# RWKV-7's chain of states: one product on TensorE's whole array for both heads of a pair

## The chip, the cores and the metric

The kernel runs on one core of a Trainium2 chip. It uses TensorE (PE: matrix products, with its weight loads PEld), VectorE (DVE), ScalarE (ACT), GpSimd (POOL) and SyncE (SP, which issues most transfers). The metric is the device time of one execution in microseconds (us), lower is better, as a median over runs.

## The reference

Two decoder layers work on 256 tokens of 2048 features. Each layer normalises, projects, runs four token mixers side by side (retention, HGRN2, mLSTM, RWKV-7; 8 heads of 64 features each), projects their joined outputs back, and then runs a SwiGLU sub-layer. The change concerns RWKV-7, whose state is one 64 x 64 matrix per head:

```python
def step(state, inp):
    rt, lwt, kt, vt, kkt, at = inp
    state = (state * jnp.exp(lwt)[:, :, None, :]
             - jnp.einsum('bhvk,bhk->bhv', state, kkt)[..., None] * (at * kkt)[:, :, None, :]
             + vt[..., None] * kt[:, :, None, :])
    return state, jnp.einsum('bhvk,bhk->bhv', state, rt)
...
_, y = lax.scan(step, jnp.zeros((b, h, d, d), r.dtype), xs)
```

## The kernel before

**Large products.** Features lie on partitions, tokens on the free axis. Weights stream in from memory in units (`w_raw`, 512 KB); ACT copies each unit's high part (`w_hi`) and DVE subtracts to get the low part (`w_lo`), three units ahead of use. TensorE adds three partial products of high and low parts in PSUM. In a mixing sub-layer the input projection runs first (banks `acc`, operand `u`). Then comes the output projection, whose operands `m` are the high and low parts of the mixers' results `mx`. It takes the results in the order of `MIXED`: `rw0, hg0, ml0, hg1, ml1, rt0, rt1, rw1`. Its first three column groups, 512 wide, go through all eight results together, so that none of the later columns can start before the last results are there.

**Between the large products** `interleave` puts the steps of the mixers: it counts TensorE's own work in `self.pe`, and a step that yields `RLAT` (2.2) is put behind that much other work. The tile scheduler then sets each engine's final order with a timeline of its own. Every engine goes through its order strictly, so a product whose input is late holds up all that stand behind it on TensorE.

**RWKV-7** works on pairs of heads, four pairs per layer, one after the other; the heads of a pair lie on partitions 0 to 63 and 64 to 127 (`half[0]`, `half[1]`). `rw_head` prepares a pair while the pair before it is still at work. `rwkv` takes four chunks of 64 tokens at once up to an inverse of a 64 x 64 triangular block per head and chunk: pairwise products (`pr<-KVR,BK`), inverses of 16 x 16 blocks on DVE with three transfers through memory (`LD`, `XD`; the result is `TDD`), and products that merge them (`pr<-TDD,LoT` and so on) into `TT`. Then the states go from chunk to chunk, for n = 0 to 3:

- kappa step (n > 0): the state `S0[n]` times the chunk's kappa, which lies in `KVR` (`pr<-S,KVR`), added to `MV` by DVE into `F[4]`;
- inverse step: `TT[n]` times that (`pr<-F,TT`; for n = 0, where no state is there yet, `pr<-ra,TT`), written negated into `KVT` as -U, one head by ACT and one by DVE;
- KBT step (n < 3): `KBT[n]` times `KVT[n]` (`pr<-KVT,KBT`), decayed into `S0[n+1]` by DVE with the decayed old state `S0c` from POOL.

Each of these products is issued once per head, with 64 columns of weights; the two land on the two halves of the partitions of one PSUM bank (`R`, two banks in turn, `pr` in the profile). Last come the outputs (`pr<-KVT,G` and `pr<-S,KVR`, also under that name), copied into `kap`, and `rw_tail`: layer norm of each head (reduce, four squares on ACT, a power on POOL, four scalings on DVE), two transposes (`pr<-ident,kap`), gate product (`pr<-SG,gup`), result `mx`, split into `m` by ACT and DVE. All these products are float32; the large ones are float32r. Every product goes through `mm`, line 299, so in the profile they are told apart by their tiles.

Of the kernel before, what the change touches and what calls it, by code (L numbers as in the profile page):

```python
"""Two-layer decoder trunk: four parallel token mixers (retention, HGRN2, mLSTM, RWKV-7) and SwiGLU.

Features of the projections lie on partitions, tokens on the free axis; the residual stream has
tokens on partitions.  Large products split both float32 operands exactly into a high and a low
12-bit part and add the three significant partial products in PSUM.
"""
# [14 lines left out]
AF = mybir.ActivationFunctionType  # L21
ALU = mybir.AluOpType
# [9 lines left out]
# TensorE time (us) that other work fills before the next dependent step of a chain is put in its order  # L32
# [14 lines left out]
# ---------------------------------------------------------------- host layout  # L47
# [6 lines left out]
def _block_cols():  # L54
    """Columns of w_in for each block of 256, in the order the kernel walks them."""
    out = {}
    rw, ml, hg, rt = RW0, ML0, HG0, RET0
    out["lora"] = list(range(rw + 1536, rw + 1792))
    for s in range(2):
        out[f"rwv{s}"] = _tile_cols(rw + 1024, 2 * s) + _tile_cols(rw + 1024, 2 * s + 1)  # L60
    for j in range(4):
        out[f"rw{j}"] = _tile_cols(rw, j) + _tile_cols(rw + 512, j)
        out[f"ml{j}"] = _tile_cols(ml, j) + _tile_cols(ml + 512, j)
        out[f"hg{j}"] = _tile_cols(hg, j) + _tile_cols(hg + 512, j)
        out[f"rt{j}"] = _tile_cols(rt, j) + _tile_cols(rt + 512, j)
    for s in range(2):
        out[f"mlv{s}"] = list(range(ml + 1024 + 256 * s, ml + 1280 + 256 * s))
        out[f"mlo{s}"] = list(range(ml + 1536 + 256 * s, ml + 1792 + 256 * s))
        out[f"hgv{s}"] = list(range(hg + 1024 + 256 * s, hg + 1280 + 256 * s))
        out[f"hgg{s}"] = list(range(hg + 1536 + 256 * s, hg + 1792 + 256 * s))  # L70
        out[f"rtv{s}"] = list(range(rt + 1024 + 256 * s, rt + 1280 + 256 * s))
        out[f"rtg{s}"] = list(range(rt + 1536 + 256 * s, rt + 1792 + 256 * s))
    return out
# [147 lines left out]
# ---------------------------------------------------------------- the program  # L221


class Weights:
    """Streams weight units: load, then split into high and low parts, ahead of their use."""
# [45 lines left out]
class Trunk:  # L271
# [4 lines left out]
    # ---- small helpers  # L276
# [28 lines left out]
    def pw(self, out, a, e):  # L305
        """out = a ** e on GpSimd; e is one of the constant columns."""
        col = {-0.5: self.mhalf}[e]
        n = a.shape[1]
        self.lp = self.nc.gpsimd.tensor_tensor(out=out, in0=a, in1=col.to_broadcast([128, n]), op=ALU.pow)  # L309
# [9 lines left out]
    # ---- setup  # L319
# [49 lines left out]
    # ---- plan of the weight stream  # L369
# [36 lines left out]
    # ---- large products  # L406
    def u_slice(self, k):
        """High and low parts of a feature chunk."""
        u = self.u[k // 2][:, k % 2]
        return u[:, 0, :], u[:, 1, :]  # L410

    def ft_unit(self, acc, k0):
        """Four feature chunks of a block with features on partitions."""
# [11 lines left out]
    def gu_unit(self, accs, k0):  # L425
        """Four feature chunks of a gate and up block, a bank each; the products with the low part apart."""
# [13 lines left out]
    def tf_block(self, accs, ncol=256):  # L440
        """A block with tokens on partitions, a bank for each half of them."""
# [12 lines left out]
    def y_acc(self, bank, bank2=None, wide=False):  # L454
        """Places of the two token halves of a block: one bank, or one each."""
# [3 lines left out]
    def y_unit(self, acc, xs, k0, last):  # L459
        """Adds a weight unit from chunk k0 on; returns the next chunk."""  # L460
# [18 lines left out]
    def halves(self, acc):  # L479
        """A wide block as two of 256 columns."""  # L480
        return [(tuple(o[:, c:c + 256] for o in acc[0]), True) for c in (0, 256)]

    # ---- norms
# [48 lines left out]
    def behind_norm(self):  # L532
        """Keeps work that is ready early out of the norm's way."""
# [5 lines left out]
    def y_stats(self, acc, b, which, yw, final=False):  # L539
        """Scaled block of the sub-layer's output and its shares of the three sums."""  # L540
# [66 lines left out]
    # ---- feed-forward sub-layer  # L607
# [54 lines left out]
    # ---- mixing sub-layer  # L662
# [3 lines left out]
    def mixing(self):  # L666
        tc, nc, A, l = self.tc, self.nc, self.A, self.l
        with ExitStack() as ctx:
# [16 lines left out]
            with self.behind_norm() if l > 0 else nullcontext():  # L685
# [4 lines left out]
                # parameters derived on chip: 1 - mu for the fourteen shifted tiles, 1 - k_a, HGRN bounds  # L690
# [10 lines left out]
                # shared scratch  # L701
# [20 lines left out]
    # ---- order of TensorE's work in the mixing sub-layer  # L722
    def interleave(self):
        """The stream of large products runs through; a step of a mixer goes in between as soon as what
        it waits for should be there.  Times are estimates in microseconds of TensorE's own work."""
# [33 lines left out]
    def stream(self):  # L759
        """Projections, then the output products as far as their inputs are there."""  # L760
# [54 lines left out]
    def settle(self):  # L815
        """Empty the finished blocks whose destinations are free; split finished mixer outputs."""
# [90 lines left out]
    # ---- pieces the mixers share  # L907
    def ssq(self, sq, ps):
        """Per-token, per-head sums of a [feature, token] tile: ps[token, (half, head)]."""
# [3 lines left out]
    def widen(self, rc, rb):  # L913
        """Repeat rc[token, (half, head)] over the features of the head."""
# [12 lines left out]
    def finish(self, j, scale_fn, out):  # L927
        """Normalise each head of the attended values, weigh and gate it."""
# [12 lines left out]
    def attend(self, P, v, j, nw=None):  # L941
        """Sum over source tokens, [feature, token] of the pair's heads; kept squared and weighed."""
# [12 lines left out]
    def scores(self, q, k, hh):  # L955
        """k^T q of one head: [source, (first|second target half of the first source half, second half)]."""
# [6 lines left out]
    def oth_tiles(self, t):  # L963
# [12 lines left out]
        # running maxima, a row for each head: high parts from row 0, low parts from row 32  # L976
# [11 lines left out]
    # ---- retention  # L988
# [48 lines left out]
    # ---- HGRN2  # L1037
    def hgrn_bounds(self, t):
        """Second layer's lower bounds: (p0 + p1) - p0 of the softmax over layers."""
# [39 lines left out]
    def hgrn(self, j, st, v, out):  # L1079
        """Scores by levels: a target in the upper half of 2m tokens meets the sources of the lower half,  # L1080
        both decayed to the middle.  The queries of the pair's heads stand side by side in q2, each on
        its head's features, with zeros on the other's."""
# [4 lines left out]
        # scores within blocks of 64 (source, target) gather in the middle of P, then move to its sides  # L1087
# [7 lines left out]
        e = out  # L1095
# [58 lines left out]
    # ---- mLSTM  # L1154
# [15 lines left out]
    def ml_stats(self):  # L1170
        """Stabiliser quantities of all heads: g = i - F, running maximum M of g and 0, exp(-(F + M))."""
# [44 lines left out]
    def mlstm(self, j, qk, v, out):  # L1216
# [14 lines left out]
        # values and the normaliser (the column of ones) with tokens on partitions  # L1231
# [31 lines left out]
    # ---- RWKV-7  # L1263
    def shift(self, acc, ct, mu, i, out):
        """Mix each token's projection with the one before it."""
# [16 lines left out]
    def vmix(self):  # L1282
        """Mix the first layer's values into this one's."""
# [17 lines left out]
    def rw_tiles(self, t):  # L1301
# [11 lines left out]
        self.TT = t([128, 4, 64], "TT")  # L1313
# [12 lines left out]
    def decay(self, th, p):  # L1326
        """exp(-DECAY * sigmoid(x)) in place from th = tanh(x / 2): (e^-DECAY/4 * exp(z))^2, z = -DECAY/4 * th."""
# [14 lines left out]
    def rw_head(self, j):  # L1342
        """What a pair needs of its projections; runs while the pair before it goes through its states."""
# [15 lines left out]
        # keys of unit length: their squared lengths divide b, where both of its keys come together  # L1359
# [31 lines left out]
    def rwkv(self, j, out):  # L1391
# [8 lines left out]
        for hh in range(2):  # L1400
            self.mul(KVR[half[hh], :, hh, :], c4(kap[half[hh]]), cpd[half[hh], :, 0:64])
            self.act(KVR[half[hh], :, 1 - hh, :], c4(vj[half[hh]]))
        self.mul(KVR[:, :, 2, :], c4(r), cpd[:, :, 1:65])
        yield RWB
        # pairwise products within chunks, rows b (own half) and k (other half), columns kappa and r
# [16 lines left out]
        # token-major copies  # L1422
# [6 lines left out]
        # merge to 32 x 32 and 64 x 64 inverses: products of both heads  # L1429
# [10 lines left out]
        # inverses of the 16 x 16 diagonal blocks, one block per partition  # L1440
# [24 lines left out]
        def quad_mm(lhs, rhs, up):  # L1465
            """32 x 32 products; the results land on the upper (0) or lower (1) rows of each half."""
# [16 lines left out]
        self.tt(TT, TT1, pair_mm(lambda i, n, h: Q[i, n, :], lambda i, n, h: TT1[i, n, :]), ALU.subtract)  # L1483
# [6 lines left out]
        a, b = quad_mm(lambda n, h: T2[bot[h], n, lo], lambda n, h: TT[bot[h], n, hi], 0)  # L1490
        self.act(TT[top[0], :, hi], a, AF.Copy, scale=-1.0)
        self.ts(TT[top[1], :, hi], b, -1.0)
        yield RLAT
        RS = F[4][:, 0:64]
        # states from chunk to chunk; KVT's kappa rows become -U
        S0 = self.S0
        for n in range(4):
            rs = MV[:, n, :]
            if n > 0:
                ps = self.ret_bank()  # L1500
                for hh in range(2):
                    self.mm(ps[half[hh], 0:64], KVR[half[hh], n, hh, :], S0[half[hh], n, :])
# [4 lines left out]
            for hh in range(2):  # L1507
                self.mm(ps[half[hh], 0:64], TT[half[hh], n, :], rs[half[hh]])
# [7 lines left out]
            for hh in range(2):  # L1516
                self.mm(ps[half[hh], 0:64], KBT[:, n, hh, :], KVT[:, n, hh, :])
            if n == 0:
                self.ts(S0[:, 1, :], ps[:, 0:64], ce)
            else:  # L1520
                self.ts(self.S0c, S0[:, n, :], ce, eng=nc.gpsimd)
                self.stt(S0[:, n + 1, :], ps[:, 0:64], ce, self.S0c)
            yield RLAT
        # outputs with tokens on partitions, a bank for each head
# [11 lines left out]
    def rw_tail(self, j, out):  # L1536
        """Layer norm of each head and the output gate."""
# [50 lines left out]
```

## Time and profile before

| | us |
|---|---|
| median of 3 runs | 2700.67 |
| the runs | 2698.83, 2700.67, 2704.54 |
| span of the profiled execution | 2700.2 |
| PE busy in it | 2655.1 |
| DVE busy | 1689.8 |
| ACT busy | 1300.0 |

The profiled execution's own time is not listed beside its span; the span, from its first to its last instruction, is 0.5 us under the median. The first layer's mixing takes about the first 600 us, its SwiGLU sub-layer goes on to 1345, the second layer's mixing to 1941, and its SwiGLU sub-layer to the end. A row of a group or of the timeline names line, engine, operation, output tile <- input tiles, for a product the stationary size (rows*columns), the moving size, and the count of records; in the timeline the start and the length in us come first, and in brackets an idle time before it with what ended it. Records of TensorE overlap: what one costs is read from how much later the next starts.

### The profile page before, as it was taken

What the parts mean: (1) busy time and instruction counts of PE and PEld (TensorE: products, weight loads), DVE (VectorE), ACT (ScalarE), POOL (GpSimd) and SP (SyncE); (2) the same over time, 40 slices, a digit from 0 to 9 for tenths busy, and PEclk for the clock granted to TensorE, in tenths of its full rate; (3) what the DMA queues carried; (4) which work ended last, traced back from release to release, by engine and by line L of the source; (5) the groups of instructions that cost most, each with busy time, mean ns of one, the idle gap of its engine ahead of it and who ended that gap; (6) DMA issues with size and microseconds to landing.
All of it is one profiled execution on the core that took longest, in us unless ns stands there. A gap on an engine that the chain in (4) does not pass through costs nothing.

```text
span 2700.2 us, 45134 instructions
## 1 busy us (share of the span) xinstructions
PE 2655.1 (98%) x17892; PEld 2356.6 (87%) x17892; DVE 1689.8 (63%) x2993; ACT 1300.0 (48%) x2146; POOL 60.4 (2%) x125
## 2 busy tenths in 40 slices
PE   7999999999999999999999999999999999999998
PEld 7989899888888888888999898997888888888888
DVE  6776867576555555545578678675765555554444
ACT  5454444456444444444464544444664444444442
POOL 0000000000000000000000000000000000000000
PEclk9999999999999999999999999999999999999999
DMA  6544344555556666666545443444556666566664
GB/s 226 160 132 135 112 151 133 158 174 173 188 189 189 189 188 187 194 197 197 190 152 157 131 130 113 150 140 145 172 186 188 188 188 188 188 188 193 198 202 142
DMA packets 149461, 459.06 MB, mean 170 GB/s; under 512 B 29121, under 2 KB 40065, under 8 KB 149249
## 3 DMA queue, kind: packets, MB, share of 16 engines
q1 hardware_dynamic: 148576, 455.51, 53.7%
q8 instruction: 140, 2.29, 0.3%
q10 hardware_dynamic: 672, 0.66, 0.1%
q14 instruction: 73, 0.59, 0.1%
HBM read 450.61 MB, written 3.41 MB: 168 GB/s over the span
## 4 chain that ended last, share of the span: by engine, by line
PE 96%; DVE 2%; DMA 1%; ACT 0%; issue 0%; SPq 0%; POOL 0%; POOLq 0%; DVEq 0%; ACTq 0%
PE acc L299 54%; PE po L299 28%; PE pr L299 13%; PE po L303 0%; PE pr L303 0%; DVE h L291 0%; DVE w_lo L247 0%; DMA A<-A 0%; DMA XD<-kap 0%; DMA h<-in_x 0%; DMA F<-LD 0%; DVE un L287 0%; DVE A L278 0%; DMA F<-XD 0%; POOL small L309 0%
## 5 line engine op out<-in xcount | busy, mean ns | idle before, releaser
L247 DVE TENSOR_TENSOR w_lo<-w_raw,w_hi 128x1024 fp32r<-128x1024 f32 x840 | 1027.9, 1224 | 763.0 <-ACT w_hi L246 756.9
L246 ACT ACTIVATE w_hi<-w_raw 128x1024 fp32r<-128x1024 f32 x840 | 888.9, 1059 | 1025.7 <-PE acc L299 372.4
L299 PE MATMUL acc<-u,w_hi 128*128 128x256 f32 (+1 forms) x4256 | 1004.4, 316 | 2.2 <-DVE u L291 1.1
L299 PEld LDWEIGHTS acc<-u,w_hi 128*128 128x128 f32 x4256 | 702.1, 191 | 61.1 <-issue 4.0
L299 PE MATMUL acc<-u,w_lo 128*128 128x256 f32 x2656 | 751.4, 285 | 0.7 <-DVE w_lo L247 0.7
L299 PEld LDWEIGHTS acc<-u,w_lo 128*128 128x128 f32 x2656 | 506.2, 191 | 9.1 <-DVE w_lo L247 0.9
L299 PE MATMUL po<-u,w_hi 128*128 128x512 f32 x1056 | 383.9, 396 | 0.0
L299 PE MATMUL po<-u,w_lo 128*128 128x256 f32 x1056 | 289.6, 279 | 0.0
L299 PE MATMUL pr<-u,w_hi 128*128 128x512 f32 x704 | 245.7, 396 | 0.0
L299 PEld LDWEIGHTS po<-u,w_hi 128*128 128x128 f32 x1056 | 196.5, 188 | 44.4
L299 PEld LDWEIGHTS po<-u,w_lo 128*128 128x128 f32 x1056 | 199.0, 188 | 3.6
L299 PE MATMUL pr<-u,w_lo 128*128 128x256 f32 x704 | 192.6, 279 | 0.0
L299 PE MATMUL acc<-w_hi,ah 128*128 128x256 f32 (+1 forms) x528 | 177.4, 336 | 0.0
L299 PE MATMUL acc<-w_lo,ah 128*128 128x256 f32 (+1 forms) x528 | 177.4, 336 | 0.0
L299 PE MATMUL acc<-w_hi,al 128*128 128x256 f32 (+1 forms) x528 | 177.4, 336 | 0.0
L299 PEld LDWEIGHTS pr<-u,w_hi 128*128 128x128 f32 x704 | 130.4, 188 | 29.5
L299 PE MATMUL acc<-w_hi,u 128*128 128x256 f32 (+1 forms) x768 | 151.3, 290 | 0.0
L299 PEld LDWEIGHTS pr<-u,w_lo 128*128 128x128 f32 x704 | 132.6, 188 | 2.1
L299 PE MATMUL po<-w_hi,ah 128*128 128x512 f32 (+1 forms) x352 | 127.6, 362 | 0.0
L299 PE MATMUL po<-w_hi,al 128*128 128x512 f32 (+1 forms) x352 | 127.6, 362 | 0.0
L299 PE MATMUL po<-w_lo,ah 128*128 128x512 f32 (+1 forms) x352 | 127.6, 362 | 0.0
L299 PEld LDWEIGHTS acc<-w_hi,u 128*128 128x128 f32 x768 | 120.7, 190 | 4.6 <-issue 2.2
(287 smaller groups left out, 2949.9 us busy)
## 6 DMA issues: line engine op xcount, KB each, us to landing
w_raw<-in_wgu SPq DMA_DIRECT2D x352, 512.0 KB, 4.6
w_raw<-in_win SPq DMA_DIRECT2D x240, 512.0 KB, 3.9
w_raw<-in_wdn SPq DMA_DIRECT2D x132, 512.0 KB, 4.1
w_raw<-in_wout SPq DMA_DIRECT2D x48, 512.0 KB, 3.5
w_raw<-in_wdnn SPq DMA_DIRECT2D x44, 512.0 KB, 3.4
w_raw<-in_woutn SPq DMA_DIRECT2D x16, 512.0 KB
w_raw<-in_wmv SPq DMA_DIRECT2D x8, 544.0 KB, 3.9
bp<-in_bpost SPq DMA_DIRECT2D x32, 128.0 KB, 3.5
```

Source lines behind the costliest of these rows:

```text
L246: self.nc.scalar.activation(hi, t, AF.Copy)
L247: self.nc.vector.tensor_tensor(out=lo, in0=t, in1=hi.bitcast(F32), op=ALU.subtract)
L299: self.nc.tensor.matmul(out, lhsT=lhsT, rhs=rhs, start=start, stop=stop, skip_group_check=True)
```

## The change

- `TT`, the inverse, gets room for both heads side by side: `[128, 4, 2, 64]`, head 0 in the first 64 columns of its partitions, head 1 in the last 64, zeros elsewhere (a block diagonal of 128 x 128 for each chunk). GpSimd clears it once in a layer.
- `KD`, a new tile of the same shape, holds kappa of chunks 1 to 3 in the same way, copied from `KVR` by ACT, one copy per head.
- The kappa and the inverse step become one product each, of 128 rows and 128 columns of weights for 64 moving columns. The KBT step becomes one product of 128 columns with 128 moving columns, of which only the two diagonal blocks are used.
- The writes that made `TT` and `S0` for both heads at once now go head by head: two subtractions for `TT`; for `S0[1]` one ACT and one DVE operation, for later chunks two on DVE.
- The area of SBUF that is reserved for descriptors of transfers is set to 1024 bytes per partition.

```diff
-        self.TT = t([128, 4, 64], "TT")
+        self.TT, self.KD = t([128, 4, 2, 64], "TT"), t([128, 4, 2, 64], "KD")
+        for x in (self.TT, self.KD):
+            nc.gpsimd.memset(x, 0.0)
...
             self.act(KVR[half[hh], :, 1 - hh, :], c4(vj[half[hh]]))
+            self.act(self.KD[half[hh], 1:4, hh, :], KVR[half[hh], 1:4, hh, :])
...
-        self.tt(TT, TT1, pair_mm(lambda i, n, h: Q[i, n, :], lambda i, n, h: TT1[i, n, :]), ALU.subtract)
+        p = pair_mm(lambda i, n, h: Q[i, n, :], lambda i, n, h: TT1[i, n, :])
+        for hh in range(2):
+            self.tt(TT[half[hh], :, hh, :], TT1[half[hh]], p[half[hh]], ALU.subtract)
...
-        a, b = quad_mm(lambda n, h: T2[bot[h], n, lo], lambda n, h: TT[bot[h], n, hi], 0)
-        self.act(TT[top[0], :, hi], a, AF.Copy, scale=-1.0)
-        self.ts(TT[top[1], :, hi], b, -1.0)
+        a, b = quad_mm(lambda n, h: T2[bot[h], n, lo], lambda n, h: TT[bot[h], n, h, hi], 0)
+        self.act(TT[top[0], :, 0, hi], a, AF.Copy, scale=-1.0)
+        self.ts(TT[top[1], :, 1, hi], b, -1.0)
...
-                for hh in range(2):
-                    self.mm(ps[half[hh], 0:64], KVR[half[hh], n, hh, :], S0[half[hh], n, :])
+                self.mm(ps[:, 0:64], self.KD[:, n].rearrange("p s t -> p (s t)"), S0[:, n, :])
...
-            for hh in range(2):
-                self.mm(ps[half[hh], 0:64], TT[half[hh], n, :], rs[half[hh]])
+            self.mm(ps[:, 0:64], TT[:, n].rearrange("p s t -> p (s t)"), rs)
...
-            for hh in range(2):
-                self.mm(ps[half[hh], 0:64], KBT[:, n, hh, :], KVT[:, n, hh, :])
-            if n == 0:
-                self.ts(S0[:, 1, :], ps[:, 0:64], ce)
+            self.mm(ps[:, 0:128], KBT[:, n].rearrange("p s t -> p (s t)"), KVT[:, n].rearrange("p s t -> p (s t)"))
+            own = [(h, ps[h, 64 * hh:64 * hh + 64]) for hh, h in enumerate(half)]
+            if n == 0:
+                self.act(S0[half[0], 1, :], own[0][1], AF.Copy, scale=ce[half[0]])
+                self.ts(S0[half[1], 1, :], own[1][1], ce[half[1]])
             else:
                 self.ts(self.S0c, S0[:, n, :], ce, eng=nc.gpsimd)
-                self.stt(S0[:, n + 1, :], ps[:, 0:64], ce, self.S0c)
+                for h, p in own:
+                    self.stt(S0[h, n + 1, :], p, ce[h], self.S0c[h])
...
-    nc = bacc.Bacc("TRN2", target_bir_lowering=False, num_devices=1)
+    nc = bacc.Bacc("TRN2", target_bir_lowering=False, num_devices=1, dynamic_dma_scratch_size=1024)
```

The scheduler also orders the program anew. Two places follow. The first is TensorE's order at the third KBT step of pair 0 in the first layer; `acc1` is a block of the weight stream. Before:

```order
L299 MATMUL pr1_89<-KVT_323,KBT_324 64x64
L299 MATMUL acc1_86<-u_199,w_hi_2231 128x256 x2
L299 MATMUL acc1_86<-u_199,w_lo_2232 128x256
L299 MATMUL acc1_86<-u_211,w_hi_2261 128x256 x2
L299 MATMUL acc1_86<-u_211,w_lo_2262 128x256
...
L299 MATMUL pr1_89<-KVT_323,KBT_324 64x64
L299 MATMUL acc1_86<-u_211,w_hi_2261 128x256 x2
```

The two heads' products stood apart, with stream products between. Now:

```order
L299 MATMUL acc1_86<-u_211,w_lo_2263 128x256
L299 MATMUL acc1_86<-u_211,w_hi_2262 128x256 x2
L299 MATMUL pr1_89<-KVT_323,KBT_324 128x128
L299 MATMUL acc1_86<-u_211,w_lo_2263 128x256
L299 MATMUL acc1_86<-u_211,w_hi_2262 128x256 x2
```

One product stands in the place of the two. The second place is TensorE's order at the end of the second layer's mixing, around the transposes of pair 3's result. Before, where `m_18797` and `m_18800` are the parts of `ml1` and `rt0`:

```order
L299 MATMUL po0_90<-w_lo_19036,m_18797 128x512
L299 MATMUL acc1_86<-w_hi_19053,m_18800 128x512 x2
L299 MATMUL acc2_87<-w_hi_19053,m_18800 128x512 x2
L299 MATMUL acc1_86<-w_lo_19054,m_18800 128x512
L299 MATMUL acc2_87<-w_lo_19054,m_18800 128x512
L299 MATMUL acc1_86<-w_hi_19053,m_18800 128x512 x2
L299 MATMUL acc1_86<-w_lo_19054,m_18800 128x512
L299 MATMUL acc2_87<-w_hi_19053,m_18800 128x512 x2
L303 MATMUL pr0_88<-ident_111,kap1_13287 128x128 x2
L299 MATMUL acc2_87<-w_lo_19054,m_18800 128x512
```

Pair 3's transposes stood among the products of `rt0`. Now, where `m_18774` and `m_18800` are the parts of `rt0` and `rt1`:

```order
L299 MATMUL po0_90<-w_lo_19064,m_18774 128x512
L299 MATMUL pr0_88<-S0_13290,KD_13287 128x64
L299 MATMUL pr1_89<-F4_13270,TT_13286 128x64
L299 MATMUL pr0_88<-KVT_13281,G_13283 64x64
...
L299 MATMUL pr1_89<-S0_13290,KVR_13279 64x64
L299 MATMUL pr1_89<-SG_13268,gup_13236 128x256
L303 MATMUL pr0_88<-ident_111,kap1_13274 128x128 x2
L299 MATMUL acc1_86<-w_hi_19081,m_18800 128x512
L299 MATMUL acc2_87<-w_hi_19081,m_18800 128x512
L299 MATMUL acc0_85<-w_hi_19099,m_18800 128x512
```

All products of `rt0` stand ahead of pair 3's last kappa and inverse step; the outputs (left out) and the transposes follow without a weight product between, and then come the products of `rt1`. The splits of the results stand at the same time in ACT's order, now as follows, with `m_18777` that of `rw1`, which holds pair 3's result:

```order
L294 ACTIVATE F3_13269,rwc1_13295<-kap1_13274,rwc1_13295 128x64 x4
L294 ACTIVATE m_18777<-mx_13342 128x2x256
L294 ACTIVATE m_18800<-mx_13341 128x2x256
L246 ACTIVATE w_hi_19135<-w_raw_19097 128x1024
```

The split of `rt1` stands behind that of `rw1`, as it did before (there with four weight splits between the squares and them). In the first layer the transposes of pair 3 still stand among the products of `rt0`.

## The prediction

> **What bounds the kernel now.** First the busy shares, then the chain that ended last, then what TensorE (PE) waited for.
>
> ```profile
> PE 2655.1 (98%) x17892; PEld 2356.6 (87%) x17892; DVE 1689.8 (63%) x2993; ACT 1300.0 (48%) x2146; POOL 60.4 (2%) x125
> PE 96%; DVE 2%; DMA 1%; ACT 0%; issue 0%; SPq 0%; POOL 0%; POOLq 0%; DVEq 0%; ACTq 0%
> ...
> PE po L303 <- DVE un L287: 27.5, 5, 13.5
> PE pr L299 <- DVE TDD L278: 1.5, 1, 1.5
> ```
>
> PE is 96% of the chain, and apart from the norms (27.5 us in 5 waits) its longest wait is one of 1.5 us. So the mixing stages are PE's own work, and what a product costs PE is what the kernel pays, until a wait shows. The products that are joined (name, stationary size, moving size, records) and their nearest full-array relatives:
>
> ```profile
> L299 PE MATMUL pr<-S,KVR 64*64 64x64 f32 x192 | 23.5, 242 | 0.0
> L299 PE MATMUL pr<-F,TT 64*64 64x64 f32 x96 | 8.0, 243 | 0.0
> L299 PE MATMUL pr<-KVT,KBT 128*64 128x64 f32 x96 | 13.5, 246 | 0.0
> L299 PE MATMUL po<-mlv,P 128*128 128x65 f32 x96 | 11.7, 270 | 0.0
> ```
>
> A plain float32 product has two records (48 products of KVT and KBT, 96 records). The mean of a record hides overlap, so a price is read from the timeline: how much later the weight stream goes on.
>
> ```profile
> 163.27 0.28 PE L299 MATMUL acc<-u,w_lo 128*128 128x256 f32 x1
> 163.47 0.33 PE L299 MATMUL pr<-F,TT 64*64 64x64 f32 x4
> 163.74 0.50 PE L299 MATMUL acc<-u,w_hi 128*128 128x256 f32 x2
> 164.08 0.28 PE L299 MATMUL acc<-u,w_lo 128*128 128x256 f32 x1
> 164.19 0.40 PE L299 MATMUL acc<-u,w_hi 128*128 128x256 f32 x2
> 164.43 0.28 PE L299 MATMUL acc<-u,w_lo 128*128 128x256 f32 x1
> ...
> 179.18 0.28 PE L299 MATMUL acc<-u,w_lo 128*128 128x256 f32 x1
> 179.39 0.33 PE L299 MATMUL pr<-KVT,KBT 128*64 128x64 f32 x2
> 179.65 0.50 PE L299 MATMUL acc<-u,w_hi 128*128 128x256 f32 x2
> 179.99 0.28 PE L299 MATMUL acc<-u,w_lo 128*128 128x256 f32 x1
> ...
> 237.10 0.28 PE L299 MATMUL acc<-w_lo,u 128*128 128x256 f32 x1
> 237.22 0.33 PE L299 MATMUL po<-mlv,P 128*128 128x65 f32 x2
> 237.36 0.48 PE L299 MATMUL acc<-u,w_hi 128*128 128x256 f32 x2
> 237.68 0.28 PE L299 MATMUL acc<-u,w_lo 128*128 128x256 f32 x1
> ```
>
> From one w_lo product to the next the stream alone takes 0.36 us (164.08 to 164.43). With both heads' TT products between it takes 0.81 (163.27 to 164.08): price 0.45. With one head's KBT product alone it also takes 0.81: price 0.45. So two heads side by side cost no more than one head, and a step whose heads stand apart pays twice. The full-array product of 65 columns takes 0.58 (237.10 to 237.68): price 0.22. The difference is at the edges: 0.20 us passes before a part-array product (163.27 to 163.47), 0.12 before the full one.
>
> [...]
>
> **Joining the products (a gain).** Per layer and pair there are 3 kappa, 4 inverse and 3 KBT steps, 80 in all. In TensorE's program order all 24 kappa steps and the 24 later inverse steps have their heads together; the 8 first inverse steps and 17 of 24 KBT steps have them apart.
> - Kappa: 24 x (0.45 - 0.22) = 5.5 us.
> - Later inverse steps: the same, 5.5.
> - First inverse steps: 8 x (2 x 0.45 - 0.22) = 5.4.
> - KBT: the joined product moves 128 columns. It lies between 65 columns (0.22) and 256:
>
> ```profile
> 143.19 0.42 PE L299 MATMUL acc<-w_hi,u 128*128 128x272 f32 x2
> 143.44 0.29 PE L299 MATMUL acc<-w_lo,u 128*128 128x272 f32 x1
> 143.57 0.42 PE L299 MATMUL acc<-w_hi,u 128*128 128x272 f32 x2
> 143.82 0.60 PE L299 MATMUL po<-A,A 128*128 128x256 f32 x2
> 144.07 0.47 PE L299 MATMUL acc<-w_lo,u 128*128 128x272 f32 x1
> 144.38 0.41 PE L299 MATMUL acc<-w_hi,u 128*128 128x272 f32 x2
> ```
>
> There 0.81 us (143.57 to 144.38) stand for the stream's 0.38 (143.19 to 143.57): price 0.43. Between 0.22 and 0.43 I take 0.24, near the lower end, since half of 0.43 is the floor's 0.22 again. Then 7 x 0.21 + 17 x 0.66 = 12.7; at 0.43 it would be 8.
> - The order changes elsewhere too: the stream is broken into 364 times instead of 408. 25 of the 44 are the steps above; the other 19 are worth 0 to 0.19 each (0.45 less the 0.26 of the product itself). I take 2.
>
> Sum: 31 us, with ends 24 and 33.
>
> **What is added, behind PE.**
>
> ```profile
> L294 ACT ACTIVATE KVR<-v 64x256 f32<-64x256 f32 x16 | 6.6, 410 | 0.1
> ```
>
> Per pair: two KD copies on ScalarE (ACT), at most 0.41 each by the larger copy of v into KVR; a second subtraction for TT on VectorE (DVE), 0.42 at most; one more S0 update per chunk, 0.28 at most. That is under 1 us of ACT and 1.3 us of DVE per pair in some 110 us, on engines busy 48% and 63%: cost 0, with PE's queue as the cover. Uncovered, 8 pairs would pay up to 17 us. The first chunk's S0 now needs ACT as well, which can stand behind a weight split of 1.06 us; a kappa step is 3 us of stream later in the order. POOL clears TT and KD once a layer, before any product reads them, and is busy 2%. No DMA is moved, and the smaller reserved area serves none of the queues listed: cost 0.
>
> **A new wait (a loss), at the end of the second layer's mixing.** There the new order, shown under the change, puts pair 3's last kappa step, last inverse step, outputs and transposes next to each other with no weight product between, and the products after them need m of rt1, whose split stands on ACT behind that of pair 3's result. Before, the transposes stood among the products of rt0. What was hidden, from the timeline:
>
> ```profile
> 1884.42 0.29 DVE L1533 COPY kap<-pr 128x128 f32<-128x128 f32 x1 [3.21 <-PE pr L299]
> ...
> 1885.76 0.41 DVE L1542 TENSOR_REDUCE rwc<-kap 128x4 f32<-128x256 f32 x1
> ...
> 1888.21 1.04 POOL L309 TENSOR_TENSOR rwc<-rwc,mhalf 128x4 f32<-128x4 f32 x1 [34.97 <-DVE rwc L287]
> ...
> 1890.05 0.98 DVE L287 TENSOR_SCALAR kap<-kap,rwc 128x64 f32<-128x64 f32 x4
> ...
> 1895.60 0.38 PE L303 MATMUL pr<-ident,kap 128*128 128x128 f32 x2
> ...
> 1896.53 0.42 DVE L278 TENSOR_TENSOR mx<-F,pr 128x256 f32<-128x256 f32 x1
> 1896.99 1.15 ACT L294 ACTIVATE m<-mx 128x512 fp32r<-128x512 f32 x2
> ```
>
> - Kappa to outputs: VectorE's share of U stands behind the split of the weight unit whose buffer is freed just ahead. A split is w_hi then w_lo (1.06 and 1.22 us), then 0.23 for U:
>
> ```profile
> L246 ACT ACTIVATE w_hi<-w_raw 128x1024 fp32r<-128x1024 f32 x840 | 888.9, 1059 | 1025.7 <-PE acc L299 372.4
> L247 DVE TENSOR_TENSOR w_lo<-w_raw,w_hi 128x1024 fp32r<-128x1024 f32 x840 | 1027.9, 1224 | 763.0 <-ACT w_hi L246 756.9
> L286 DVE TENSOR_SCALAR KVT<-pr 64x64 f32<-64x64 f32 x32 | 7.3, 228 | 5.2 <-ACT KVT L294 4.5
> ```
>
>   2.5 us, less about 0.2 of products: 2.3. If the split is done in time, about 1.
> - Outputs to transposes: the copy 0.29, then 1885.76 to 1889.25 for reduce to power, then 0.98, less 0.4 for the gate product that stands there: 4.4.
> - Transposes to the first product: 1895.60 to 1898.14, 2.5.
>
> 9.2 us in all. Such idle time lowers the clock:
>
> ```profile
> 1900.00:1960.00 60.00, 54.79 (x345) 49.19 (x344) 46.09 (x110) 36.54 (x92) 1.70 (x2) 0.94 0.53 164
> ```
>
> This window holds the norm's wait; 0.06 x 60 = 3.6 us of clock are lost in it, part of them while PE is idle anyway. I add 1.5 (0 to 3.6). [...]
>
> **The inverse blocks.** The only RWKV wait of before, 1.5 us on TDD, is pair 2's in the first layer. Between that pair's last BK product and its first LoT product the new order has 27 fewer stream products (3.2 us), but VectorE has two w_lo splits fewer in that stretch (2.4 us). The wait grows by 0 to 3.2; I take 1.5.
>
> **Sum.** -31 + 9.2 + 1.5 + 1.5 = -18.8 us against the span of 2700.2, so 2681.4. The median of the runs, 2700.67, is 0.5 above the span: I forecast 2682.
>
> **Rivals.**
> - The waits are small: U's split is in time, the clock term and TDD cost nothing, and the 19 other breaks count in full. -33 + 8 = -25: 2676, and 2668 if nothing of the wait shows. For it: at other steps of the chain PE comes 2 to 4 us after the data. Chance 0.22.
> - The joined product costs what the two heads together cost (0.45), because tiles that ran side by side lose nothing. Then only the 25 split steps gain: 25 x 0.45 = 11, which the 12 us of waits take back: 2701, no change. [...] Chance 0.08.
> - Slower: the chain of pairs becomes the bound through the inverse blocks. Each pair's wait for TDD costs PE one to one once the blocks come later than now; 31 us of gain less 12 of waits are used up when each of the 8 pairs waits 2.4 us more, and at 3.5 us more the time is 2682 + 28 = 2710. The added DVE and ACT work is 2 us per pair, mostly outside that stretch. Chance 0.04.
>
> **Chances.** My forecast has 0.66, with its own range 2674 to 2690 (waits of 5 to 20 us). The range 2667 to 2694 takes in the first rival and KBT's dear end. 0.2% is 5.4 us, about what can be told from no change: faster (below 2695.3) 0.66 + 0.22 = 0.88, same 0.08, slower 0.04.
>
> **What would show it.** Right: 160 fewer PE records; pr<-S,KD and pr<-F,TT as 128*128 with 0.22 us of delay; a PE idle time of 7 to 11 us near the end of the second layer's mixing, put down to kap, mx or m, with the granted clock below 1 there; none in the first layer's. Wrong: delays of 0.4 us or more at the joined products, TDD waits in many pairs, or no idle time before m.

## The result, and the profile after

The changed kernel takes 2681.22 us (median of 4 runs, 2680.21 to 2681.69) against 2702.11 for the kernel before on the same chip: a ratio of 0.9925, 95% interval 0.9913 to 0.9938. The forecast was 2682 in a range of 2667 to 2694. The span of the profiled execution went from 2700.2 to 2679.7, 20.5 us less. Nearly all of it comes from the two mixing stages: the transposes of the norm that ends a stage begin 15.3 us earlier after the first layer's mixing (601.7 before, 585.8 now, with the start of the program 0.6 earlier). About 1 us of that is lost again over the SwiGLU stage, and the second layer's mixing brings only 5.9 more.

The busy times on the page of the changed kernel:

```profile
PE 2630.9 (98%) x17732; PEld 2352.7 (88%) x17732; DVE 1698.9 (63%) x3017; ACT 1308.2 (49%) x2169; POOL 67.2 (3%) x129
```

PE has 160 records fewer, as 80 joined products of two records each must give, and 24.2 us less busy time. DVE and ACT have 9.1 and 8.2 us more. 24.2 less busy and 20.5 less span means that PE's idle time grew by 3.7 us. Where, the waits of PE tell (what waited, what it waited for, total, times, longest):

```profile
PE pr L303 <- DVE kap L287: 3.2, 1, 3.2
PE acc L299 <- ACT m L294: 2.2, 1, 2.2
```

These two are new, and with them two short ones on F and kap (0.31 and 0.38 us, in the timeline below): together 6.15 us. The norm's waits are within 0.4 us of what they were. The wait for TDD, 1.5 us before, is gone. The groups of the joined products in the changed kernel (stationary size, moving size, records, busy time in us and mean length in ns, idle time before; the 16 records of the first inverse steps, `pr<-ra,TT`, come on top):

```profile
L299 PE MATMUL pr<-KVT,KBT 128*128 128x128 f32 x48 | 9.4, 277 | 0.0
L299 PE MATMUL pr<-F,TT 128*128 128x64 f32 x48 | 8.2, 252 | 0.3 <-DVE F L278 0.3
L299 PE MATMUL pr<-S,KD 128*128 128x64 f32 x48 | 8.0, 248 | 0.0
```

Their price, as in the prediction, is read from the timeline. A kappa step, then a KBT step of the changed kernel, each with the stream's products around it:

```profile
158.88 0.28 PE L299 MATMUL acc<-u,w_lo 128*128 128x256 f32 x1
...
159.23 0.33 PE L299 MATMUL pr<-S,KD 128*128 128x64 f32 x2
...
160.17 0.28 PE L299 MATMUL acc<-u,w_lo 128*128 128x256 f32 x1
...
177.38 0.28 PE L299 MATMUL acc<-u,w_lo 128*128 128x256 f32 x1
...
177.74 0.38 PE L299 MATMUL pr<-KVT,KBT 128*128 128x128 f32 x2
...
178.67 0.28 PE L299 MATMUL acc<-u,w_lo 128*128 128x256 f32 x1
```

Three periods of the stream lie between the first and the last row of each; they alone take 3 x 0.36 = 1.08 us, and both stretches take 1.29. So the price is 0.21 to 0.22 us for 64 moving columns and for 128 alike, and the inverse steps that stand alone in the stream cost the same. Before, it was 0.45 for two heads side by side and 0.45 again for each head that stood apart.

The four new waits all lie at the end of the second layer's mixing. PE's timeline of the changed kernel there:

```profile
1865.77 0.40 PE L299 MATMUL po<-w_lo,m 128*128 128x512 f32 x1
1866.01 0.33 PE L299 MATMUL pr<-S,KD 128*128 128x64 f32 x2
1866.65 0.43 PE L299 MATMUL pr<-F,TT 128*128 128x64 f32 x2 [0.31 <-DVE F L278]
1867.02 0.33 PE L299 MATMUL pr<-KVT,G 128*64 128x64 f32 x2
...
1868.04 0.34 PE L299 MATMUL pr<-KVT,G 128*64 128x64 f32 x4
...
1868.60 0.33 PE L299 MATMUL pr<-KVT,G 128*64 128x64 f32 x2
...
1869.62 0.48 PE L299 MATMUL pr<-KVT,G 128*64 128x64 f32 x4
...
1870.89 1.22 PE L299 MATMUL pr<-SG,gup 128*128 128x256 f32 x2 [0.38 <-DVE kap L1540]
1875.36 0.66 PE L303 MATMUL pr<-ident,kap 128*128 128x128 f32 x2 [3.25 <-DVE kap L287]
1878.23 1.65 PE L299 MATMUL acc<-w_hi,m 128*128 128x512 f32 x3 [2.21 <-ACT m L294]
...
1880.96 0.63 PE L299 MATMUL acc<-w_hi,m 128*128 128x512 f32 x1
1881.38 0.63 PE L299 MATMUL acc<-w_lo,m 128*128 128x512 f32 x1
...
1883.40 0.40 PE L299 MATMUL acc<-w_lo,m 128*128 128x512 f32 x1
1883.64 0.63 PE L299 MATMUL acc<-w_hi,m 128*128 128x512 f32 x2
```

After m has come, the 512-wide products follow each other at 0.42 us (1880.96 to 1881.38); from 1883.40 on they do so at 0.23. The clock that was granted to TensorE says the same (PEclk, 1 is full speed; window, length, busy time and records of PE, PEld, DVE, ACT and POOL, then PEclk, share of time that the DMA engines were busy, GB/s):

```profile
1860.00:1870.00 10.00, 9.69 (x58) 7.62 (x57) 4.70 (x7) 3.67 (x5) 0.00 (x0) 0.98 0.60 168
1870.00:1880.00 10.00, 4.16 (x12) 2.60 (x11) 4.23 (x12) 2.58 (x10) 1.04 (x1) 0.50 0.11 42
1880.00:1890.00 10.00, 10.00 (x38) 8.04 (x38) 2.50 (x3) 3.18 (x3) 0.00 (x0) 0.84 0.19 54
```

### The profile page after: what moved, and what is told of

Same layout as the page of the kernel before. It is cut to its first block, busy times and chain, and to the rows that moved or that the text cites. A ratio compares the mean times of both kernels' runs of the same rounds, so it can differ in the third digit from the quotient of the medians.

```text
span 2679.7 us, 44884 instructions
## 1 busy us (share of the span) xinstructions
PE 2630.9 (98%) x17732; PEld 2352.7 (88%) x17732; DVE 1698.9 (63%) x3017; ACT 1308.2 (49%) x2169; POOL 67.2 (3%) x129
## 4 chain that ended last, share of the span: by engine, by line
PE 98%; DVE 1%; ACT 0%; DMA 0%; issue 0%; POOL 0%; SPq 0%; POOLq 0%; DVEq 0%; ACTq 0%
PE acc L299 56%; PE po L299 28%; PE pr L299 13%; PE pr L303 1%; PE po L303 1%; DVE h L291 0%; DMA h<-in_x 0%; DVE un L287 0%; POOL small L309 0%; SPq L340 0%; ACT junk L294 0%; DVE w_lo L247 0%; DVE u L291 0%; DVE small L291 0%; DVE yw L291 0%
```

## The experiments

All ratios are to the kernel before on the same chip, in the same session (medians 2699.97, 2700.44 and 2700.94 in three sessions).

| run | median us | ratio (95%) |
|---|---|---|
| changed kernel again | 2680.89 | 0.9931 (0.9917 to 0.9944) |
| copies into KD three times | 2670.80 | 0.9894 (0.9880 to 0.9907) |
| steps after 2.0 us | 2702.88 | 1.0013 (1.0004 to 1.0022) |
| cover put back | 2674.79 | 0.9909 (0.9895 to 0.9923) |
| kappa and inverse joined alone | 2685.11 | 0.9945 (0.9931 to 0.9958) |
| KBT joined alone | 2689.94 | 0.9961 (0.9948 to 0.9973) |
| joined in rows, half the columns | 2695.61 | 0.9980 (0.9972 to 0.9989) |
| before, KBT's heads together | 2694.26 | 0.9980 (0.9971 to 0.9989) |
| copies into KD twice | 2681.42 | 0.9926 (0.9911 to 0.9941) |
| copy into KD by DVE | 2672.41 | 0.9895 (0.9878 to 0.9911) |
| small reserved area alone | 2700.63 | 0.9999 (0.9989 to 1.0008) |

### Which products bring the gain

The first question is whether the gain belongs to the joined products, and to which.

**Kappa and inverse joined, KBT as before.** The changed kernel with KBT's part taken back:

```diff
-            self.mm(ps[:, 0:128], KBT[:, n].rearrange("p s t -> p (s t)"), KVT[:, n].rearrange("p s t -> p (s t)"))
-            own = [(h, ps[h, 64 * hh:64 * hh + 64]) for hh, h in enumerate(half)]
+            for hh in range(2):
+                self.mm(ps[half[hh], 0:64], KBT[:, n, hh, :], KVT[:, n, hh, :])
...
-                for h, p in own:
-                    self.stt(S0[h, n + 1, :], p, ce[h], self.S0c[h])
+                self.stt(S0[:, n + 1, :], ps[:, 0:64], ce, self.S0c)
```

> Only the kappa and the inverse step are joined; the KBT step is issued per head as before. In the order no step of pair 3 is uncovered at the end of either layer; 21 of the 24 KBT steps have their heads apart (17 before). Theory (a part-array pair costs 0.45 us together, 0.90 apart, a full product 0.22): -5.5 -5.5 -5.4 +1.8 = -14.6 us and up to 3 more from other breaks: 2685 to 2688 us. Rival (a joined product costs as much as the pair, only steps that stood apart gain): 8 x 0.45 = 3.6 less 1.8: 2700 us.

It took 2685.11, a gain of 15.3 us, as the theory had it.

**KBT joined alone.** The kernel before with the change's KBT step, S0 writes and reserved area:

```diff
-            for hh in range(2):
-                self.mm(ps[half[hh], 0:64], KBT[:, n, hh, :], KVT[:, n, hh, :])
+            self.mm(ps[:, 0:128], KBT[:, n].rearrange("p s t -> p (s t)"), KVT[:, n].rearrange("p s t -> p (s t)"))
+            own = [(h, ps[h, 64 * hh:64 * hh + 64]) for hh, h in enumerate(half)]
...
-                self.stt(S0[:, n + 1, :], ps[:, 0:64], ce, self.S0c)
+                for h, p in own:
+                    self.stt(S0[h, n + 1, :], p, ce[h], self.S0c[h])
```

> Only the KBT step is joined. In the order no step of pair 3 is uncovered; 8 of the 24 kappa steps now have their heads apart (none before). Theory: 7 x 0.23 + 17 x 0.68 = 13.2 less 8 x 0.45 = 3.6, so -9.6 us and up to 3 more from other breaks: 2689 to 2692 us. Rival as for the kappa and inverse steps: 17 x 0.45 = 7.7 less 3.6: 2698 us.

It took 2689.94, a gain of 10.5 us, again as the theory had it. The two parts give 15.3 + 10.5 = 25.8 us, more than the 19 to 21 of the changed kernel, and neither shows a wait for kap or m. (In their orders 4 more KBT steps and 8 kappa steps have their heads apart, which costs them part of what joining brings.) That fits a changed kernel whose end takes some of the gain back; the second group of runs tests it.

**Is it the number of products or the shape?** In the next kernel kappa and inverse still read the block diagonals' 128 rows, but each head's 64 columns by a product of its own:

```diff
-                self.mm(ps[:, 0:64], self.KD[:, n].rearrange("p s t -> p (s t)"), S0[:, n, :])
+                for hh in range(2):
+                    self.mm(ps[half[hh], 0:64], self.KD[:, n, hh, :], S0[:, n, :])
...
-            self.mm(ps[:, 0:64], TT[:, n].rearrange("p s t -> p (s t)"), rs)
+            for hh in range(2):
+                self.mm(ps[half[hh], 0:64], TT[:, n, hh, :], rs)
```

> The changed kernel, but the kappa and the inverse step are two products again, each with all 128 rows and 64 columns of weights (the blocks of zeros are still multiplied). What is kept is the joined KBT step. The order leaves pair 3 uncovered at the end of the second layer, as in the changed kernel. Theory (an array that is used in part costs the edges, however many rows are used): 48 x 0.23 + 7 x 0.68 + 0.23 = 16 us slower than the changed kernel, 2697 us. Rival (what counts is that all rows are used): 0.22 a step stays, within 3 us of the changed kernel.

It took 2695.61, 13 to 15 us more than the changed kernel (by the ratios and by the medians of two sessions), near the 16 of the theory and far from the 3 of the rival. The price of its kappa step, from its timeline:

```profile
159.19 0.28 PE L299 MATMUL acc<-u,w_lo 128*128 128x256 f32 x1
159.40 0.34 PE L299 MATMUL pr<-S,KD 128*64 128x64 f32 x4
...
160.00 0.28 PE L299 MATMUL acc<-u,w_lo 128*128 128x256 f32 x1
```

0.81 us (159.19 to 160.00) stand for the stream's 0.36: 0.45, as before the change, and again 0.21 us pass ahead of it. All 128 rows are not enough (0.45); what halves the price is a product that takes all 128 columns too (0.21 to 0.22 in the changed kernel). The number of products does not matter here: in the kernel before, one head's KBT product alone, 128 rows by 64 columns as well (179.39 in the prediction's rows), cost the same 0.45 as these two together.

**Heads together, not joined.** In the kernel before, each head's KBT product over both heads' U, so that the two stand side by side in all 24 steps:

```diff
-                self.mm(ps[half[hh], 0:64], KBT[:, n, hh, :], KVT[:, n, hh, :])
+                self.mm(ps[half[hh], 0:128], KBT[:, n, hh, :], KVT[:, n].rearrange("p s t -> p (s t)"))
```

> The kernel before, but each head's KBT product takes both heads' U (128 moving columns, half of the result unused), so that both become ready at once. In the order the heads of all 24 KBT steps stand together (7 before), and nothing is uncovered. Theory (heads apart pay twice; together on the part-array 0.45, or 0.55 with 128 moving columns): 17 x 0.45 = 7.7 less up to 24 x 0.1: 2694 to 2697 us. Rival (only the full array saves): 2700 to 2703 us.

It took 2694.26, a gain of 6.2 us. Its KBT step in its timeline:

```profile
178.77 0.28 PE L299 MATMUL acc<-u,w_lo 128*128 128x256 f32 x1
...
179.22 0.44 PE L299 MATMUL pr<-KVT,KBT 128*64 128x128 f32 x4
...
180.05 0.28 PE L299 MATMUL acc<-u,w_lo 128*128 128x256 f32 x1
```

Two periods of 0.36 took 1.28, so the price is 0.56: 0.11 more than with 64 columns, and less than twice 0.45. So some of KBT's gain is only that its heads no longer stand apart. The kernel with KBT joined alone saves 4.3 us more. By the prices joining should add 24 x (0.56 - 0.22) = 8.2, less 3.6 for the eight kappa steps that stand apart in that kernel, so 4.6, close to that.

**The reserved area alone**, in the kernel before:

```diff
-    nc = bacc.Bacc("TRN2", target_bir_lowering=False, num_devices=1)
+    nc = bacc.Bacc("TRN2", target_bir_lowering=False, num_devices=1, dynamic_dma_scratch_size=1024)
```

> The kernel before with the reserved area for descriptors set to 1024 bytes and nothing else; the order of the program is that of the kernel before. Theory: the area serves none of the queues, 2699 to 2702, no change. Rival, that part of the gain came from the area: a time below 2695.

2700.63 against 2700.94: no change.

### What the waits at the end of the second layer cost

**The changed kernel once more**, to see whether the waits belong to the program or to one execution. No edit.

> The changed kernel once more, as the base for the three runs beside it. Both theories: 2681 us, ratio 0.9925, PE idle for 6.1 us in four gaps between pair 3's last inverse step and the products of rt1 in the second layer.

2680.89, and 6.1 us idle in the same four places.

**An order that covers the transposes.** The scheduler's order can be moved without touching the products. Here each copy into KD is issued three times, which adds 32 ACT copies and changes nothing else in the code; in the order that comes out, pair 3's transposes stand among the products of `rt0` in both layers:

```diff
-            self.act(self.KD[half[hh], 1:4, hh, :], KVR[half[hh], 1:4, hh, :])
+            for _ in range(3):
+                self.act(self.KD[half[hh], 1:4, hh, :], KVR[half[hh], 1:4, hh, :])
```

> Each KD copy is issued three times instead of once, 32 more copies of at most 0.41 us on ACT (11 us). Nothing else in the code changes, but the scheduler's order does: the transposes of pair 3 stand among the products of rt0 again in both layers. Theory (what was missing from the full gain is the wait at the end of the second layer and the low clock behind it, and ACT's copies are hidden): faster than the changed kernel by 6 to 10 us, 2672 us, no idle time ahead of m. Rival (the wait only stands in for a chain that is late anyhow, and ACT is near the path): no faster than the changed kernel, 2681 to 2692 us, with waits elsewhere.

2670.80: with more work it is 10.1 us faster than the changed kernel beside it. PE's waits no longer name kap or m, and its idle time is 7.4 us less than in the changed kernel and its busy time 3.0 less:

```profile
PE 2627.9 (98%) x17732; PEld 2351.8 (88%) x17732; DVE 1698.6 (64%) x3017; ACT 1319.3 (49%) x2201; POOL 68.3 (3%) x129
```

Whether the copies or the order did that, the next two runs tell.

**The copies twice** (`range(2)` in the place of `range(3)`). Here the order leaves the transposes of the second layer bare, as in the changed kernel.

> The changed kernel with each copy of kappa into KD issued twice (16 more ACT copies). Theory, that the faster run with three copies came from the order of the program: this order has the stream broken into 363 times and pair 3's transposes in the second layer uncovered, as in the changed kernel, so the idle time of 6 us before kap and m stays and the time is that of the changed kernel, 2680 to 2683. Rival, that the copies themselves help, by delaying ACT: half of the step from one copy (2681) to three (2671), 2676, with shorter waits at the transposes.

2681.42, the time of the changed kernel, and its waits for kap and m are again 3.2 and 2.2 us. So copies bring nothing, and the 16 extra ones cost nothing that can be seen.

**One copy, by DVE**, with an order that covers the transposes in both layers:

```diff
-            self.act(self.KD[half[hh], 1:4, hh, :], KVR[half[hh], 1:4, hh, :])
+            self.nc.vector.tensor_copy(self.KD[half[hh], 1:4, hh, :], KVR[half[hh], 1:4, hh, :])
```

> The changed kernel with the copy of kappa into KD made by DVE instead of ACT, issued once. Its order covers the transposes of pair 3 in both layers with products of rt0, as the kernel with three copies did, and breaks the stream 374 times (that one 372). Theory: neither kap nor m shows a wait, the copies are hidden on DVE as on ACT, 2669 to 2673. Rival, that DVE, busy 63%, shows the 32 copies of some 0.2 us at the kappa steps: up to 6 us more, 2677.

2672.41, as the theory had it. (There are 16 copies, not the 32 of the rival's text, 4.5 us in all; the ratio, 0.9895 beside 0.9894 with the copies by ACT, speaks against that price too.) PE's longest waits in this kernel behind the norm's:

```profile
PE acc L299 <- DVE w_lo L247: 1.1, 1, 1.1
PE acc L299 <- DVE u L291: 0.9, 3, 0.3
PE pr L299 <- DVE TDD L278: 0.7, 1, 0.7
```

Nothing waits for kap or m.

**The cover put back by the planner's own numbers.** The splits of the results are issued in the order of `MIXED`, and a pair's key norms are put behind 10 us of stream instead of 8:

```diff
-HNRM = 8.0
+HNRM = 10.0
...
-                if self.mh[i] is None and self.left[key] == 0:
+                if self.mh[i] is None and self.left[key] == 0 and all(x is not None for x in self.mh[:i]):
```

> The changed kernel with two edits: the split of a mixer's result waits in the code for the splits ahead of it, so that rt1's no longer stands behind rw1's, and HNRM is 10 instead of 8. In the order pair 3's last inverse step stands among the products of ml1, its transposes among those of rt1. Theory: the gaps of 6.1 us and the low clock behind them go, 2671 to 2674 us. Rival (PE only meets the same lateness at another place): 2679 to 2683 us.

2674.79, 6.1 us faster than the changed kernel and 0.8 above the range that was expected; kap and m are gone from the waits, and one of 1.6 us, for the norm's scaled output (yw), has come. Whether that wait makes the difference was not tested. Three programs with different edits and a covered end lie at 2670.8, 2672.4 and 2674.8, the two with a bare end at 2681.

**The bare end in both layers.** With a shorter distance between the steps, the order leaves pair 3's transposes bare in the first layer too:

```diff
-RLAT = 2.2
+RLAT = 2.0
```

> RLAT 2.0 instead of 2.2 in the changed kernel: the chain's steps are put closer together. In the order that comes of it the transposes of pair 3 stand right ahead of the products of rt1 in both layers. Theory (the wait costs what the chain's bare length is, wherever the order uncovers it): slower than the changed kernel by 6 to 10 us, 2689 us, with a second group of gaps of 6 us in the first layer. Rival (steps closer together shorten the chain, so that less is waited for): 2675 to 2681 us.

2702.88, 22.0 us more than the changed kernel. The direction was right, the size was a clear miss: 6 to 10 us were expected. Its longer waits in PE's timeline (first layer, then second):

```profile
547.06 0.66 PE L303 MATMUL pr<-ident,kap 128*128 128x128 f32 x2 [3.24 <-DVE kap L287]
549.93 1.65 PE L299 MATMUL acc<-w_hi,m 128*128 128x512 f32 x3 [2.21 <-ACT m L294]
...
1886.04 0.49 PE L299 MATMUL pr<-KVT,KBT 128*128 128x128 f32 x2 [1.51 <-DVE KVT L286]
1887.27 0.69 PE L299 MATMUL pr<-S,KD 128*128 128x64 f32 x2 [0.74 <-DVE S L291]
1888.27 0.69 PE L299 MATMUL pr<-F,TT 128*128 128x64 f32 x2 [0.31 <-DVE F L278]
```

In the first layer the same end has appeared as in the second, with the same 3.2 and 2.2 us. By the start of the norm's transposes the first layer's mixing is 10.4 us longer than the changed kernel's (596.8 against 585.8, from starts 0.6 apart), so a bare end costs some 10 us here as well. The rest lies in the second layer, 13.6 us by the same marks (1345.5 to 1949.3 against 1334.6 to 1924.8). There the last KBT step and the step before it in the chain stand without stream work between them too, 2.6 us more of idle time, and the low clock begins earlier in the chain (the last kappa step already takes 0.69 us, where the changed kernel's took 0.33):

```profile
1880.00:1890.00 10.00, 7.12 (x32) 5.46 (x30) 4.49 (x11) 2.55 (x4) 0.44 (x1) 0.85 0.55 168
1890.00:1900.00 10.00, 5.69 (x28) 3.42 (x26) 2.64 (x10) 1.71 (x9) 1.04 (x1) 0.50 0.00 0
1900.00:1910.00 10.00, 8.46 (x25) 6.78 (x26) 2.45 (x4) 2.21 (x3) 0.00 (x0) 0.62 0.00 0
```

The clock over these 30 us falls short of full by 10.3 us (1.5 + 5 + 3.8), against 6.8 in the 30 us of the changed kernel's end. How the rest of the 13.6 us divides among smaller waits and a longer way around them was not taken apart.

## Why the prediction was right, point by point

- **The prices.** Taken at 0.45 for two heads, 0.45 for one, 0.22 for the joined product; measured 0.22 for all joined products that stand alone in the stream. KBT was mis-sized a little: 0.24 was taken for 128 moving columns, 0.22 was measured.
- **The gain of 31 us** was some 3 too large. The run with three copies has no new wait, and PE's busy time there is 27.2 us below the kernel before, 29.2 us in the median. The sum gave every one of the 80 steps the price of a step that stands alone in the stream. In the changed kernel 31 of the 80 do not: other products of the mixers stand beside them without a stream product between, and there the edge that joining saves is partly paid by the neighbour. The last section shows such a place (1.23 us against 1.19). That these 31 steps make up the whole difference is an inference, since the order changes with each edit and no run changes only them. Nor does any run measure by itself the 2 us that the sum took for the 19 other breaks.
- **Added work at no cost:** right. 16 copies by ACT or by DVE, and 16 or 32 more, changed nothing that can be told (2681.42 with 16 more beside 2680.89; 2670.80 with 32 more and 2672.41 by DVE, where the end is covered). The small reserved area costs and brings nothing (2700.63 alone against 2700.94).
- **The new wait** is where the prediction put it, with the waits for F, kap and m. Its idle time was 6.15 us, not 9.2, and a little under the 7 to 11 that were to show it. The step that failed is the first of its three, kappa to outputs, taken at 2.3 us. VectorE's timeline there, in the changed kernel:

```profile
1867.06 1.23 DVE L247 TENSOR_TENSOR w_lo<-w_raw,w_hi 128x1024 fp32r<-128x1024 f32 x1 [0.46 <-ACT w_hi L246]
1868.32 0.23 DVE L286 TENSOR_SCALAR KVT<-pr 64x64 f32<-64x64 f32 x1
```

  The split does stand ahead of U, as predicted, and U comes at 1868.55. But VectorE's share of U is head 1's alone, and the code issues head 0's outputs first. PE works on these from 1867.02 and comes to head 1's at 1868.60, 0.05 us after U. So the split was hidden behind head 0's outputs, 1.6 us of products where the prediction had taken off 0.2; what PE idled in this step is the 0.31 us for F. The second term, outputs to transposes, was taken at 4.4; PE idled 0.38 + 3.25 = 3.63, the difference being the gate product, which took 1.22 us at the low clock where 0.4 was allowed. The third, 2.5, was 2.21.
- **The low clock** was taken at 1.5 and was larger, 3 to 3.5 by the timeline: twelve 512-wide products took 5.17 us (1878.23 to 1883.40) where 12 x 0.23 = 2.76 would do at full clock, and the gate product and the transposes lost about 0.9 more (an estimate: half of their 1.22 + 0.66 us at a granted clock of 0.50). Products were dense from 1878.23 on, and the full clock came back at 1883.3, 5.1 us later.
- **Both together**, 10.7 us predicted, are 9 to 10 by these rows, and the runs agree: 10.1 us between the changed kernel and the one with three copies, 6.1 and 9.7 (by the ratios) for the other two covered orders. The two errors, 3 too much idle time and some 2 too little clock, cancelled for the most part.
- **TDD** was taken at +1.5 and came out at -1.5: the wait is gone. In that pair TDD was ready 37.1 us after the last BK product and is now ready after 32.0, while PE, with the shorter stream, asks for it 2.2 us sooner. The prediction had counted on at most 2.4 us from the fewer splits; what else brought the blocks forward was not taken apart. In the kernel with the copy by DVE, 0.7 us of it is back.
- **The rivals.** That the joined product costs as much as the pair is refuted by the prices above. That the inverse blocks become the bound is refuted by the waits: TDD appears in none of the changed kernel's rows. The rival of small waits did not happen in the changed kernel; the covered orders show what it would have given, 2670.8 to 2674.8 against the 2668 to 2676 written down.

The sum again with what was measured: PE's busy time fell by 24.2 us, which is about 27.5 of products less about 3.3 of low clock; idle time rose by 6.15 at the end, fell by 1.5 at TDD and by 0.9 in small waits. -24.2 + 3.7 = -20.5 us, against -18.8 predicted. That the forecast came so close was in part luck: a gain 3.5 us too large stood against a TDD wait 3 us too long, an end some 1.2 too dear and 0.9 of small waits that went and had not been counted.

## What to carry to other kernels

When small products are pushed into a dense stream, price them by how much later the stream goes on, not by their own length. Two part-array products that became one full-array product cost the stream 0.22 us in the place of 0.45 here, where full-array work stood on both sides; in a place with part-array products behind it nothing was saved (1.23 us against 1.19, below). Then look in the new order for the one place where the last link of a chain stands without cover: here a third of the gain went into a single such place, and a change of the order alone brought it back (2670.8 and 2672.4, both faster than the change as it was made).

## What the runs showed of the hardware that was not expected

- A product of 128 rows and 64 columns of weights pays the same 0.45 us as two blocks of 64 x 64 (kernel with half the columns). Part of it shows at the edges: 0.21 us pass ahead of such a product, 159.19 to 159.40, against 0.12 ahead of a full one, 397.44 to 397.56 below.
- 64 or 128 moving columns of a full float32 product cost the stream the same 0.22 us. In part-array products 128 columns instead of 64 cost 0.11 more (0.56 against 0.45).
- Beside part-array products a joined product need not save anything (1.23 us against 1.19 in one place). The last inverse step of one pair, followed by outputs, in the kernel with half the columns and in the changed kernel:

```profile
402.99 0.28 PE L299 MATMUL acc<-u,w_lo 128*128 128x256 f32 x1
403.11 0.28 PE L299 MATMUL acc<-u,w_hi 128*128 128x256 f32 x1
403.32 0.34 PE L299 MATMUL pr<-F,TT 128*64 128x64 f32 x4
403.49 0.28 PE L299 MATMUL pr<-KVT,G 128*64 128x64 f32 x2
...
404.18 0.28 PE L299 MATMUL acc<-u,w_lo 128*128 128x256 f32 x1
```

```profile
397.32 0.28 PE L299 MATMUL acc<-u,w_lo 128*128 128x256 f32 x1
397.44 0.28 PE L299 MATMUL acc<-u,w_hi 128*128 128x256 f32 x1
397.56 0.33 PE L299 MATMUL pr<-F,TT 128*128 128x64 f32 x2
397.82 0.33 PE L299 MATMUL pr<-KVT,G 128*64 128x64 f32 x2
...
398.55 0.28 PE L299 MATMUL acc<-u,w_lo 128*128 128x256 f32 x1
```

  From w_lo to w_lo it is 1.19 us with four half products and 1.23 with the joined one: what the joined product saves ahead of the inverse step (0.12 against 0.21), it loses behind it (0.26 against 0.17).
- The granted clock fell before PE had idled for long. In the changed kernel it is 1.00 from 1866.2 to 1869.6, and 0.50 from there to 1883.3; the four records at 1869.62 already take 0.48 us, where the four at 1868.04 took 0.34. The last 512-wide product had ended at 1866.17. In the 3.4 us between, PE was busy for 3.09 by its records, with small products alone, and had idled for 0.31. What of this lowered the clock, and how much idle time it takes, no run shows.
